# SwiGLU over 8192 x 8192: all loads and stores of the two-row tiles through one DMA queue in a fixed order

## Chip, cores, metric

One core of a Trainium2 chip. The metric is the device time of one execution in microseconds (us), the median of several. The profile is one execution taken by the hardware profiler; "span" is the time from its first to its last instruction, which is 1.7 to 1.9 us shorter than the time of that same execution.

## The reference

```python
x = np.random.randn(8192, 8192).astype(np.float32)
a, b = np.split(x, 2, axis=-1)
return a * (b / (1 + np.exp(-b)))        # out: 8192 x 4096, float32
```

Read 268.4 MB, write 134.2 MB, and do very little with it: a kernel bound by data movement.

## The kernel before

A tile is 256 rows of x, two per partition: 64 KiB per partition to load, 32 KiB to store. There are 32 tiles (`last` is 31) and three slots, each of which holds one tile; ScalarE overwrites b with silu(b), VectorE writes a * silu(b) to the front of the same slot, and the store goes out from there. So the load of tile i+3 needs the slot of tile i, and waits until the store of i has landed.

```python
    R, BUFS = 2, 3
    def load(i, c0=0, cw=R * M):
        inst = nc.sync.dma_start(
            out=slots[i % BUFS][:, c0 : c0 + cw], in_=xv[i * P : (i + 1) * P, c0 : c0 + cw])
        ...
    def store(i, c0=0, cw=R * half):
        eng = nc.scalar if i < last - 1 else nc.sync
        if i % 2 and BUFS <= i < ntiles * 3 // 4:
            eng = nc.gpsimd
        inst = eng.dma_start(
            out=ov[i * P : (i + 1) * P, c0 : c0 + cw], in_=slots[i % BUFS][:, c0 : c0 + cw])
        ...
    for i in range(BUFS):
        load(i)
    for i in range(last):
        ...                      # swiglu(i); tiles 0 to 2 in two halves
        store(i)                 # tile 0 in two pieces
        nxt = i + BUFS
        if nxt < last:
            load(nxt)
        ...                      # the last tile in halves
```

Loads are issued from SP (SyncE), three tiles ahead. Stores are issued from ACT, eleven of them from GpSimd, the last from SP. An issuing engine feeds a queue of its own, called a **ring** below; all rings are served by the same 16 DMA engines (in the profile before, the three rings took 68.6, 19.8 and 11.4% of their time).

## Time and profile before

| | before |
|---|---|
| time, median of the first three runs | 935.39 us (935.17 to 936.15) |
| span of the profiled execution | 934.2 us |
| bytes moved | 402.67 MB |
| VectorE / ScalarE busy | 30% / 24% |

Two longer windows of the steady state show how even it is. The columns are the window, its length, busy time of VectorE, ScalarE and GpSimd with their instructions, the TensorE clock, the share of time in which the 16 DMA engines were busy, and GB/s.

```profile
200.00:316.00 116.00, 34.77 (x5) 28.12 (x4) 1.06 (x2) 1.00 1.00 434
780.00:896.00 116.00, 34.77 (x5) 28.12 (x4) 0.00 (x0) 1.00 1.00 434
```

Share 1.00 and 434 GB/s early and late. The next view is the same table for the last microseconds of the span. A DMA share of 0.06 there is one engine of sixteen. (A packet counts in the window in which it starts, so a short window can exceed 1.)

```profile
928.00:930.00 2.00, 0.00 (x0) 0.00 (x0) 0.00 (x0) 1.00 1.07 459
930.00:932.00 2.00, 0.00 (x0) 0.00 (x0) 0.00 (x0) 1.00 0.71 303
932.00:934.00 2.00, 0.00 (x0) 0.00 (x0) 0.00 (x0) 1.00 0.02 8
```

Nearly all engines stop within two microseconds of one another: from 1.07 to 0.71 to 0.02.

### The profile page before, as it was taken

How to read it: one execution, taken by the hardware profiler on the slowest of the kernel's cores; microseconds unless marked ns; L12 is line 12 of the kernel's file. 1: busy time of each engine (PE TensorE's matmuls, PEld its weight loads, DVE VectorE, ACT ScalarE, POOL GpSimd, SP SyncE). 2: the span in 40 equal slices, each digit the busy share in tenths (PEclk: the TensorE clock that was granted, in tenths of full speed). 3: DMA queues.
4: the chain of work that ended last, by engine and by line, in shares of the span. 5: the costliest groups of instructions: out<-in, count | busy, mean ns of one | idle time of the engine just before them, and what ended most of it. 6: DMA issues, size and time to landing. Idle time of an engine off the chain costs nothing.

```text
span 934.2 us, 219 instructions
## 1 busy us (share of the span) xinstructions
DVE 278.8 (30%) x37; ACT 226.8 (24%) x38; POOL 6.2 (1%) x15
## 2 busy tenths in 40 slices
DVE  0333123332133321333213333133331233312342
ACT  0412320333202333023330233311333113331141
POOL 0000000000000000000000000000000000000000
DMA  9999999999999999999999999999999999999998
GB/s 404 418 426 434 427 441 450 432 427 429 446 414 441 428 443 431 428 434 459 429 413 460 410 446 428 428 446 427 428 429 464 408 429 446 428 446 428 427 428 382
DMA packets 9649, 402.67 MB, mean 431 GB/s; under 512 B 1072, under 2 KB 1072, under 8 KB 1200
## 3 DMA queue, kind: packets, MB, share of 16 engines
q1 hardware_dynamic: 5184, 276.83, 68.6%
q10 hardware_dynamic: 2880, 79.69, 19.8%
q0 software_dynamic: 1584, 46.14, 11.4%
q14 instruction: 1, 0.01, 0.0%
HBM read 268.44 MB, written 134.22 MB: 431 GB/s over the span
## 4 chain that ended last, share of the span: by engine, by line
DMA 70%; issue 12%; DVE 9%; ACT 7%; DVEq 0%; POOL 0%; SPq 0%; POOLq 0%
DMA slot<-in_x_dram 38%; DMA out_dram<-slot 32%; DVE slot L70 9%; ACT slot L66 7%; DVEq L138 0%; POOL out_dram L79 0%; SPq L55 0%; POOLq L79 0%; DVEq L70 0%
## 5 line engine op out<-in xcount | busy, mean ns | idle before, releaser
L70 DVE TENSOR_TENSOR slot<-slot 128x8192 f32<-128x8192 f32 (+2 forms) x37 | 278.8, 7539 | 641.5 <-ACT slot L66 641.2
L66 ACT ACTIVATE slot<-slot 128x8192 f32<-128x8192 f32 (+2 forms) x37 | 225.5, 6105 | 690.1 <-DMA slot<-in_x_dram 690.1
L79 POOL DMA_DIRECT2D out_dram<-slot x11 | 6.0, 544 | 695.6 <-DVE slot L70 695.6
L66 ACT ACT_TABLE_LOAD x1 | 1.3, 1283 | 0.7 <-PEq L127 0.7
L127 POOL MEMSET const-bfloat16-1.0<- 128x1 bf16 x1 | 0.1, 102 | 0.0
L127 POOL MEMSET const-float32-0.0<- 128x1 f32 x1 | 0.1, 99 | 0.2 <-issue 0.2
L127 POOL MEMSET const-float32-1.0<- 128x1 f32 x1 | 0.1, 99 | 0.0
L127 POOL MEMSET const-uint8-127<- 128x1 uint8 x1 | 0.1, 99 | 0.0
## 6 DMA issues: line engine op xcount, KB each, us to landing
out_dram<-slot ACTq DMA_DIRECT2D x18, 4096.0 KB, 32.8
out_dram<-slot POOLq DMA_DIRECT2D x11, 4096.0 KB, 32.6
slot<-in_x_dram SPq DMA_DIRECT2D x2, 4096.0 KB, 29.8
out_dram<-slot SPq DMA_DIRECT2D x1, 4096.0 KB, 19.3
out_dram<-slot SPq DMA_DIRECT2D x2, 2048.0 KB, 14.5
out_dram<-slot ACTq DMA_DIRECT2D x1, 3584.0 KB, 37.5
out_dram<-slot ACTq DMA_DIRECT2D x1, 512.0 KB, 24.6
slot<-in_x_dram SPq DMA_DIRECT2D x31, 38.4
```

Of the source, the lines that this page charges most:

```text
L66: gate = nc.scalar.activation(out=b, in_=b, func=_SILU)
L70: prod = nc.vector.tensor_mul(out=o[:, k0:k1, c0 : c0 + cw], in0=a, in1=b)
L79: inst = eng.dma_start(out=ov[i * P : (i + 1) * P, c0 : c0 + cw], in_=slots[i % BUFS][:, c0 : c0 + cw])
L127: nc = _bacc.Bacc("TRN2", target_bir_lowering=False, num_devices=1)
```

## The change

The intent: fix the order of all transfers by putting them in one ring, as load i+1, store i, load i+2, store i+1, so that each load is followed by the store whose data is ready, and no ring competes with it. The last three stores stand behind the last loads. The special cases for GpSimd and for tile 0 go, and loads run two tiles ahead in place of three.

```diff
     def store(i, c0=0, cw=R * half):
-        eng = nc.scalar if i < last - 1 else nc.sync
-        if i % 2 and BUFS <= i < ntiles * 3 // 4:
-            eng = nc.gpsimd
-        inst = eng.dma_start(
+        inst = nc.sync.dma_start(
...
-    for i in range(BUFS):
-        load(i)
+    load(0)
+    load(1)
     for i in range(last):
...
+        if i == last - 1:
+            swiglu(last, 0, 1)
+        if i + 2 == last:
             load(last, 0, M)
             load(last, M, M)
+        store(i)
+        if i + 2 < last:
+            load(i + 2)
```

More of the change, by code (lines that the diff above doesn't have):

```diff
@@ L59, in load, with swiglu @@
         loads[i].append(inst)
-    def swiglu(i, k0=0, k1=R, c0=0, cw=half, gated=None):
+    def swiglu(i, k0=0, k1=R, c0=0, cw=half):
         rows = slots[i % BUFS].rearrange("p (k s c) -> p k s c", k=R, s=2)
@@ L67, in swiglu @@
         follows_from_others(gate, i, [], [loads, gates, prods, stores])
-        if gated:
-            gated()
         prod = nc.vector.tensor_mul(out=o[:, k0:k1, c0 : c0 + cw], in0=a, in1=b)
@@ L83, in store @@
         stores[i].append(inst)
-    for i in range(BUFS):
-        load(i)
+    load(0)
+    load(1)
     for i in range(last):
-        if i == 0:
-            swiglu(i, 0, 1)
-            swiglu(i, 1, 2, gated=lambda: store(0, 0, half // 4))
-            store(i, half // 4, R * half - half // 4)
-        elif i < BUFS:
+        if i < BUFS:
             for k in range(R):
                 swiglu(i, k, k + 1)
-            store(i)
         else:
             swiglu(i)
-            if i == last - 1:
-                swiglu(last, 0, 1)
-            store(i)
-        nxt = i + BUFS
-        if nxt < last:
-            load(nxt)
-        elif nxt == last:
+        if i == last - 1:
+            swiglu(last, 0, 1)
+        if i + 2 == last:
             load(last, 0, M)
             load(last, M, M)
+        store(i)
+        if i + 2 < last:
+            load(i + 2)
     store(last, 0, half)
```

## The prediction

> **What bounds the kernel now.** I read the head of the profile page first: engine shares, DMA row, traffic.
>
> ```profile
> span 934.2 us, 219 instructions
> ...
> DVE 278.8 (30%) x37; ACT 226.8 (24%) x38; POOL 6.2 (1%) x15
> ...
> DMA  9999999999999999999999999999999999999998
> ...
> DMA packets 9649, 402.67 MB, mean 431 GB/s; under 512 B 1072, under 2 KB 1072, under 8 KB 1200
> ```
>
> VectorE is busy 30% and ScalarE 24%. The DMA engines are at nine tenths or more in 39 of 40 slices, and in the last slice at eight. The question is whether "nine tenths" hides a gap that a better order of transfers could close. So next I took the table of windows for single periods of the steady state (columns: window, its length, busy time of VectorE, ScalarE and GpSimd, clock, DMA share, GB/s).
>
> ```profile
> 200.00:229.00 29.00, 8.69 (x2) 7.03 (x1) 0.00 (x0) 1.00 1.00 434
> 229.00:258.00 29.00, 8.68 (x2) 7.03 (x1) 0.53 (x1) 1.00 1.00 434
> 258.00:287.00 29.00, 8.70 (x2) 7.03 (x1) 0.00 (x0) 1.00 1.00 434
> ```
>
> One tile (a load of 8.39 MB, a store of 4.19 MB) takes 29.0 us, and in it the DMA share is 1.00: there is no gap. 12.58 MB in 29.0 us is 434 GB/s. The timeline confirms the period (columns: start, duration, engine, instruction, in brackets the idle time before it):
>
> ```profile
> 192.48 7.03 ACT L66 ACTIVATE slot<-slot 128x8192 f32<-128x8192 f32 x1 [21.97 <-DMA slot<-in_x_dram]
> 199.54 8.69 DVE L70 TENSOR_TENSOR slot<-slot 128x8192 f32<-128x8192 f32 x1 [20.31 <-ACT slot L66]
> 208.26 0.34 ACTq L79 DMA_DIRECT2D out_dram<-slot  x1
> 221.48 7.03 ACT L66 ACTIVATE slot<-slot 128x8192 f32<-128x8192 f32 x1 [21.97 <-DMA slot<-in_x_dram]
> ```
>
> 221.48 - 192.48 = 29.0 us between activations, of which ScalarE waits 22 for the load. The compute chain from a landed load to a finished product is 7.03 + 8.69, about 15.8 us, half a period.
>
> Last I read the trace's packet records, since shares round. Starts and ends can be strung into 16 strands of serial packets, one per DMA engine. A 64 KiB load packet takes 2.418 us and the next begins about 4 ns before it ends (spacing 2.414); a 32 KiB packet, load or store, takes 1.213 (spacing 1.209); a 16 KiB packet has spacing 0.607, a 4-byte semaphore packet 0.006. From the first packet to the last, about 930.0 us, only one strand has any gap over 30 ns, of 0.3 us. So the bound is the **16 DMA engines' packet rate**, and they never lack work. The long chain of waits (load, ScalarE, VectorE, store, load) is a consequence: each DMA in it is slow because the engines are shared.
>
> **What the Trainium skill says.** "DMA: Bandwidth & Descriptors", section "Issuing engines are not separate DMA queues", says that DMAs issued from ACT, SP and GpSimd run on the same 16 engines and interleave, and that issuing from several saves only sequencer time. The trace agrees: a 32 KiB store packet takes 1.213 us on the ACT, the GpSimd and the SP queue alike. Section "Where 436 GB/s comes from" puts the ceiling at 435.2 GB/s; the steady state measures 434, so at most 0.3% is left. Section "Queues, rings and completion order" says that an engine alternates between rings at packet boundaries; the strands do show load and store packets taking turns. It also says that a completion increment lands only after every earlier write of that engine, and "DMA engines do not wait on semaphores". That matters below.
>
> **The change, part by part.** The bytes, packets, compute instructions and three slots stay.
>
> *Packet work per engine.* Each transfer gives an engine 8 packets. After: 31 loads x 8 x 2.414 = 598.7; the last load in halves, 16 x 1.209 = 19.3; 31 stores x 8 x 1.209 = 299.8; the last store in halves, 16 x 0.607 = 9.7; some 66 semaphore packets x 0.006 = 0.4. Sum **927.9 us**. Before differs only in store 0, sent in pieces: 8 x (0.155 + 1.058) = 9.71 in place of 9.67, a saving of 0.04. On top each engine now loses about 1.6 us to slow packets: 0.7 on the very first, 0.7 at about 55 us. 927.9 + 1.6 = 929.5, against about 930.0 seen. The rest of the span, 934.2 - 930.0 = 4.2 us, is start (the first load is issued at 0.74 and packets flow about 1.4 later) and end (one engine finishes 1.2 after the median, then about 0.9 to the last instruction).
>
> *Issues moved.* 20 issues leave ACT (0.34 each), 11 leave GpSimd (0.53 each). Both wait for loads or products most of the time, so that is worth nothing.
>
> *The single queue: does it run dry?* Its order is load i+1, store i, load i+2, store i+1. Alone on the engines a load lasts 19.3 us (8 packets), a store 9.7. Let load i land at T. Then store i-1 runs to T + 9.7 and load i+1 to T + 29.0. Store i is issued when its product is done, T + 15.8, and its turn comes at T + 29.0: **13 us early**. Load i+2 stands behind it, and needs store i-1 (same slot), landed by about T + 9.7 + 2 = T + 11.7 (the 2 is an estimate, from start latency). So it goes out right after store i, at T + 16.2, 22 us before its turn. No wait reaches the engines.
>
> *Start.* Two loads are issued instead of three. Load 0 lands at 22.6 as before; load 1 keeps the engines until about 42. Store 0 is issued whole after both half products, whose end can be read in the chain of waits before: 30.84 + 4.44 = 35.3. Plus 1.5 to flow is 37, 5 us ahead of need. This is the thinnest margin.
>
> *End.* After the last load only stores 29, 30 and 31 are left, 29 us of transfers, while the products of the last half take about 7 us after its load. No gap, but before had none either, so nothing is gained.
>
> *Sum.* Work -0.04; slow packets between -0.7 (if the stall at 55 us, which falls at the moment ACT issued store 1 at 55.26, goes away) and +0.5; the straggler at the end +-0.5. Span 933.8. The timed median lay 1.2 over the profiled span (935.39 against 934.2), so **935.0 us**.
>
> **The rivals.**
>
> *Order becomes cost: a bubble at each boundary.* With two queues, another ring could fill an engine while one ring waits for the confirmation of its last writes; with one ring nothing fills it. Were each of some 64 boundaries to cost 0.3 us, the time would be 954, the lower edge of "slower". Against it: at the start loads 0, 1 and 2 follow one another in the SP ring alone, and the 4-byte packet between them costs 6 ns; at the end stores 30 and 31 follow load 31 in the SP ring, and the two halves of store 31 run alone there, again with no gap. Only store-then-load in one ring is never shown.
>
> *Pure phases are faster.* If mixing reads and writes cost something, stretches of loads alone and of stores alone would gain. Against: load packets at the start, with no store running, take 2.418 us just as in the mixed steady state, and store packets at the end take 1.213 as in the middle. Even without the two slow spells and with perfect ends the time stays above 932; 2% faster would be 916.7, which is 12 us below the packet sum alone. I see no way to it.
>
> *A wait of the in-order SP sequencer.* A late store now holds the load behind it back. The margins (13 us steady, 5 at the start) speak against it; missing the start's margin wholly costs a few us once, some 938.
>
> **Range and chances.** The packet sum pins the time from below (927.9 + 4.2 + 1.2 = 933.3 with no slow packet), and known run-to-run spread is 935.2 to 936.2. I take 933.2 to 937.0 for 8 in 10; the longer upper side is for small bubbles. Faster by over 2% has 0.01, slower 0.02 (the bubble rival), within 2% 0.97.
>
> **What the changed profile would show.** Steady windows of 29.0 us still at share 1.00 and 434 GB/s. Stores land about 24 us after issue instead of 32.8 (T + 15.8 to T + 39 to 40), while loads take about 42 instead of 38.4 (T + 16.2 to T + 58). SP's own waits move from stores to VectorE, about 28 us per tile, with loads waiting for stores next to nothing. ACT's idle before a gate stays near 22. Store 0 is issued at about 35.3. Wrong would be: gaps over 0.1 us between packets at the change from store to load, a share below 0.99, or packets with other durations than 2.418 and 1.213.

## The result, and the profile after

| | before | after |
|---|---|---|
| median | 935.74 us (4 runs, 935.17 to 936.15) | 940.09 us (4 runs, 939.13 to 941.92) |
| ratio | | 1.0048, 95% interval 1.0034 to 1.0062 |
| span of the profiled execution | 934.2 us | 940.1 us |

A ratio here is the mean time of one kernel's fast runs over the mean of the other's fast runs of the same rounds, so not quite the ratio of the medians. The changed kernel is 0.5% slower, 3 us above the top of the predicted range.

First the parts that came out as predicted. The timeline of one period after (start, duration, engine, instruction; in brackets the idle time before it):

```profile
249.68 7.03 ACT L66 ACTIVATE slot<-slot 128x8192 f32<-128x8192 f32 x1 [22.05 <-DMA slot<-in_x_dram]
256.74 8.69 DVE L68 TENSOR_TENSOR slot<-slot 128x8192 f32<-128x8192 f32 x1 [20.39 <-ACT slot L66]
265.46 0.34 SPq L74 DMA_DIRECT2D out_dram<-slot  x1
265.89 0.38 SPq L55 DMA_DIRECT2D slot<-in_x_dram  x1
278.87 7.03 ACT L66 ACTIVATE slot<-slot 128x8192 f32<-128x8192 f32 x1 [22.16 <-DMA slot<-in_x_dram]
```

The store leaves at T + 15.8 and the load right behind it at T + 16.2, as computed. But the period is 278.87 - 249.68 = 29.19 us in place of 29.00. From the list of DMA issues after (KB each, median us from issue to landing):

```profile
out_dram<-slot SPq DMA_DIRECT2D x31, 4096.0 KB, 23.0
slot<-in_x_dram SPq DMA_DIRECT2D x31, 42.0
```

Predicted were about 24 and 42. The waits of SP's own queue after (waited for, us in total, times, longest):

```profile
SPq L74 <- DVE slot L68: 866.4, 33, 33.6
...
SPq L55 <- DMA out_dram<-slot: 22.0, 1, 22.0
```

SP waits for products, hardly ever for stores to land, so no load is held back. The order does what it was meant to do. Now the DMA row of the page, with the lines beside it, and the tail in the windows:

```profile
DMA  9999999999999999999999999999999999999996
...
DMA packets 9505, 402.67 MB, mean 428 GB/s; under 512 B 1056, under 2 KB 1056, under 8 KB 1056
```

```profile
928.00:930.00 2.00, 0.00 (x0) 0.00 (x0) 0.00 (x0) 1.00 1.01 434
930.00:932.00 2.00, 0.00 (x0) 0.00 (x0) 0.00 (x0) 1.00 0.92 393
932.00:934.00 2.00, 0.00 (x0) 0.00 (x0) 0.00 (x0) 1.00 0.23 98
934.00:936.00 2.00, 0.00 (x0) 0.00 (x0) 0.00 (x0) 1.00 0.19 82
936.00:938.00 2.00, 0.00 (x0) 0.00 (x0) 0.00 (x0) 1.00 0.15 66
938.00:940.00 2.00, 0.00 (x0) 0.00 (x0) 0.00 (x0) 1.00 0.02 8
```

Until 932 us the row is full. Then 0.19 of the engines, 3 of 16, work alone for some 6 us. **Thirteen engines are done at the old time; three are late, and the kernel ends with the slowest.**

The packet records say why. They name no engine, but packets of one engine follow each other about 4 ns short of end to end, so they can be strung into 16 strands, each with the sequence of packets that the program gives every engine. After: thirteen strands end 930.3 to 931.6 us after the first packet, three at 935.9, 936.1 and 937.2. Before: fifteen end at 929.6 to 930.3, one at 931.2. The slowest differs by 937.2 - 931.2 = 6.0, and the spans by 940.1 - 934.2 = 5.9. That is the whole loss of this execution, which was the slowest of the four.

The late strands have no gaps. They have *stretched packets*: 64 KiB load packets that took over 20 ns longer than 2.418 us. After the first 100 us there are 74 in the trace after and 3 in the trace before, and they sit in one place, the eighth packet of a load, the one directly ahead of a store (all excess over 2.418, small ones too, after the first two turns, all strands):

```
packet of a load     1st   2nd   3rd   4th   5th   6th   7th     8th
stretch, ns in sum   489    21     1    30     8    17   518   18747
```

The delay of the slowest strand behind the median one grows fast and then slowly: 2.5 us after load 4, 3.5 after load 7, 4.8 after load 13, 5.8 after load 19, 6.6 after load 28.

Being hit goes with being late. In the traces after, e1_again and e6_all_act together, between 100 and 870 us, the last packet of a load was stretched in 171 of 404 cases in which at least 10 of the other 15 strands were already storing (counted 0.1 us before the packet's ordinary end), and in 64 of 846 cases in which fewer were. Which of the two brings about the other no run tells.

One turn does not fit. At the end, the last two loads follow one another for 38.6 us without a store between them, and stores 29 to 31 come behind them. In after, e1_again and e6_all_act no packet from 872 us of the span on was stretched by more than 15 ns, on any engine. So an unmixed turn can pass without a stall; what the steady turns have besides is open.

### The profile page after: what moved, and what is told of

Same layout as the page of the kernel before. It is cut to its first block, busy times and chain, and to the rows that moved or that the text cites. A ratio compares the mean times of both kernels' runs of the same rounds, so it can differ in the third digit from the quotient of the medians.

```text
span 940.1 us, 219 instructions
## 1 busy us (share of the span) xinstructions
DVE 278.8 (30%) x37; ACT 226.8 (24%) x38; POOL 0.2 (0%) x4
## 4 chain that ended last, share of the span: by engine, by line
DMA 72%; DVE 14%; ACT 11%; SPq 1%; issue 0%; DVEq 0%
DMA slot<-in_x_dram 69%; DVE slot L68 14%; ACT slot L66 11%; DMA out_dram<-slot 2%; SPq L74 1%; DVEq L126 0%; SPq L55 0%; DVEq L68 0%
```

## The experiments

Theory S: an engine that turns from loads to stores is stretched at the turn; hits on the same engines add up, and since each engine has a fixed share of every transfer, its delay is never given back. (The diffs are against the changed kernel unless said otherwise, and abridged.) Rivals: a disturbance of one execution; the shallower prefetch; the SP ring itself; boundaries between transfers in one ring whatever their direction; and, inside theory S, what makes a turn costly.

The table gathers what the packets of nine traces showed; the other runs are told in their sections. A ratio is taken with executions of the kernel before on the same chip in the same rounds. "Stretch per run of loads" is the lengthening of all load packets over 20 ns in the steady state (100 to 870 us), divided by the number of unbroken runs of load packets, per engine. "Late" counts strands that end over 1.5 us behind the median one.

| run | median us | ratio to before | run of loads, us | stretch per run, ns | late | slowest behind median, us |
|---|---|---|---|---|---|---|
| before | 935.74 | | mostly 2.4 | 0.0 | 0 | 1.2 |
| after | 940.09 | 1.0048 | 19.3 | 44 | 3 | 6.7 |
| e1_again | 939.63 | 1.0043 | 19.3 | 61 | 6 | 5.3 |
| e2_store_act | 936.07 | 1.0003 | mostly 2.4 | 0.1 | 0 | 0.6 |
| e3_halves | 941.59 | 1.0062 | 9.7 | 12 | 4 | 2.7 |
| e6_all_act | 940.13 | 1.0046 | 19.3 | 56 | 6 | 4.3 |
| e9_pairs_mended | 940.58 | 1.0053 | 38.6 | 79 | 6 | 4.7 |
| e11_quarters | 947.90 | 1.0130 | 4.9 | 2 | 2 | 3.4 |
| e13_two_rings_in_step | 941.72 | 1.0065 | 19.3 | 41 | 5 | 3.1 |

### Again, unaltered (e1_again)

> The changed kernel once more, unaltered. Theory S (the stall at the switch): in the one ring, the last 64 KiB packet of a load, the one just ahead of the store, is stretched on some engines; an engine hit repeatedly falls behind and ends last. Expected: 939 to 942 us, 1.003 to 1.007 of before, stretched packets (over 2.44 us) almost all the eighth of their load, two to four engines ending 5 to 7 us after the median engine. Rival N (a disturbance of that one profiled execution): the late engines are gone, or the stretched packets lie anywhere in a load.

Measured: 939.63 us, ratio 1.0043 (1.0030 to 1.0056). The tail of this run:

```profile
930.00:932.00 2.00, 0.00 (x0) 0.00 (x0) 0.00 (x0) 1.00 0.96 410
932.00:934.00 2.00, 0.00 (x0) 0.00 (x0) 0.00 (x0) 1.00 0.40 172
934.00:936.00 2.00, 0.00 (x0) 0.00 (x0) 0.00 (x0) 1.00 0.36 156
936.00:938.00 2.00, 0.00 (x0) 0.00 (x0) 0.00 (x0) 1.00 0.10 41
```

Six late engines this time (0.36 of 16), two more than "two to four", the slowest 5.3 us late. Of the 74 packets stretched after the first 100 us, 71 are the last of their load. The rival of a single disturbance falls.

### The stores back on a second ring (e2_store_act)

```diff
-        inst = nc.sync.dma_start(
+        inst = nc.scalar.dma_start(
             out=ov[i * P : (i + 1) * P, c0 : c0 + cw], in_=...
```

> The same order and the same two loads ahead, but the stores are issued from ACT, so that a second ring has work at every switch. Theory S: packets of loads and stores take turns again, no stretched packets after the first 100 us, all engines end within about 1.5 us, 934.5 to 936 us (0.999 to 1.001 of before). Rival D (two loads ahead in place of three, and the order of issue, are to blame): stays at 939 to 941 us.

Measured: 936.07 us, ratio 1.0003 (0.9991 to 1.0016). Its tail:

```profile
930.00:932.00 2.00, 0.00 (x0) 0.00 (x0) 0.00 (x0) 1.00 1.12 475
932.00:934.00 2.00, 0.00 (x0) 0.00 (x0) 0.00 (x0) 1.00 0.02 8
```

No late engine. One load packet in about 3000 runs of loads was stretched in the steady state. Order of issue and depth of prefetch are those of the changed kernel, so neither is to blame: one line undoes the loss.

### Loads in place of the stores (e4_reads)

```diff
+        if i < last - 2:
+            inst = nc.sync.dma_start(
+                out=slots[i % BUFS][:, c0 : c0 + cw], in_=xv[i * P : (i + 1) * P, c0 : c0 + cw])
+        else: ...                # the store as it was
```

> Wrong output on purpose: in tiles 0 to 28 each store is replaced by a load of the same 4 MiB into the same part of the slot, in the same place of the same ring with the same waits; only the last three stores write. Ring, boundaries, completion packets and order are kept, only the change of direction is gone. Theory S: no stretched eighth packets until the last three stores, all engines end within 1.5 us, 933 to 936 us. Rival B (the boundary between two transfers in one ring, whatever their direction): stays at 939 to 942 us with late engines.

Measured (output wrong): 936.33 us, ratio 1.0007 (0.9993 to 1.0021). Its tail:

```profile
930.00:932.00 2.00, 0.00 (x0) 0.00 (x0) 0.00 (x0) 1.00 1.01 434
932.00:934.00 2.00, 0.00 (x0) 0.00 (x0) 0.00 (x0) 1.00 0.23 98
934.00:936.00 2.00, 0.00 (x0) 0.00 (x0) 0.00 (x0) 1.00 0.00 0
```

All engines end within 0.9 us, and of 473 packets of 64 KiB at the end of a load two were stretched, by 31 and 38 ns. (After the first 100 us 40 load packets at other places were, by some 50 ns each, mostly the first or second of a load; they add up to no late engine.) The rival of the bare boundary falls: it takes a change of direction. The time was 0.3 us above the range that was expected.

### The whole ring on ACT (e6_all_act)

The edit replaces `nc.sync` by `nc.scalar` in `load` and in `store`.

> The changed kernel with every load and store on the ACT ring in place of the SP ring. If the stall belongs to one ring changing direction, whichever ring it is: 939 to 942 us with late engines and stretched eighth packets. If the SP ring or SyncE's issue is at fault: 935 to 936 us.

Measured: 940.13 us, ratio 1.0046 (1.0034 to 1.0058), six late engines; all 95 packets stretched after the first 100 us are the last of their load. The SP ring as such is not the cause.

### Half and quarter blocks (e3_halves, e11_quarters)

```diff
-        store(i)
-        if i + 2 < last:
-            load(i + 2)
+        for k in range(R):
+            store(i, k * half, half)
+            if i + 2 < last:
+                load(i + 2, k * M, M)
```

> One SP ring still, but load halves and store halves alternate: 60 switches from load to store in place of 30, and a pause between stores of 9.7 us in place of 19.3. The smaller packets alone add about 2 us by their spacing (8 x 31 x (2 x 1.209 - 2.414) + 8 x 31 x (2 x 0.607 - 1.209)). Theory S with a cost per switch: the late engines fall back about twice as far, 10 to 13 us, 944 to 950 us. Variant S2, the cost grows with the length of the pause in the stores: the lag is as before or less, 937 to 942 us.

Measured: 941.59 us, ratio 1.0062. Twice the turns, but the slowest engine is 2.7 us behind the median in place of 5.3, and the stretch per run of loads is 12 ns in place of 61. A fixed cost per turn is refuted. The time stays at the level of the changed kernel because what the shorter lag gives back, the smaller packets take: the median engine ends 934.2 us after the first packet in place of 930.6.

> One SP ring, quarters of loads and stores alternating: about 120 switches, a pause of 4.8 us between stores. The smaller packets alone add about 7 us by estimate (16 KiB packets at 0.607: 248 x (4 x 0.607 - 2.414) = 3.5; 8 KiB packets at some 0.306 each, not yet measured: 248 x (4 x 0.306 - 1.209) = 3.7). S2: no stretched last packets after the first 200 us and all engines within 2 us, 940 to 943 us. Cost per switch: late engines by over 5 us, 947 us or more.

Measured: 947.90 us, ratio 1.0130. The mechanism came out as S2 said (2 ns per run of loads), the time did not: 5 us over the expected range. The median engine ends 9.1 us later than in e1_again. Of this the packet sizes give 7.2 (the spacing of 8 KiB packets did measure 0.306), and 183 more completion packets per engine give 183 x 0.006 = 1.1, which I had left out. The end of this kernel still loads tile 31 in one run of 19.3 us and then sends store 29 whole. At that turn, 907 us after the first packet, the last one or two of the 16 load packets were stretched on all 16 engines, by 22.9 us in sum, 1.4 per engine; the first packets of that run, for which the ring had waited for a slot, had lost another 3.4 us in sum. So this one turn cost more than all the stretch of loads in the steady state before it, 3.1 us in sum. One strand ends 3.4 us behind the median; where it lost that I have not isolated. Short blocks nearly avoid the stall, and their small packets cost more than it.

### Two loads, then two stores (e5_pairs, e9_pairs_mended)

```diff
+    for i in range(0, last - 3, 2):
+        compute(i); compute(i + 1)
+        store(i);   store(i + 1)
+        load(i + 3); load(i + 4)
```

> One SP ring, but two loads and then two stores at a time: 15 switches from load to store in place of 30, and a pause between stores of 38.6 us in place of 19.3. Cost per switch: the late engines fall back half as far, 2.5 to 3.5 us, 936.5 to 938.5 us. Cost that grows with the pause (S2, which the halves point to): each stall is longer and the total is as after or more, 939 to 943 us.

Measured: 943.84 us, ratio 1.0083. The kernel had a flaw of mine at its end: load 31 waited for store 28 to land with nothing else in the ring. The windows show the hole:

```profile
880.00:885.00 5.00, 0.00 (x0) 5.00 (x1) 0.00 (x0) 1.00 0.88 380
885.00:890.00 5.00, 3.62 (x1) 1.35 (x1) 0.00 (x0) 1.00 0.14 59
```

So its time proves nothing. Its steady state does: 121 of 208 last packets stretched, 147 ns per run of loads. The mended version puts stores 28 and 29 ahead of load 31.

> The pairs again without the hole of their end (there load 31 waited for store 28 with nothing else in the ring; now stores 28 and 29 go ahead of it). Theory S2 (fewer switches, but each pause of the stores 38.6 us long, stalls summed over the engines some 2.4 us per switch as in the first pairs run): no hole, and 938.5 to 941 us, as long as the changed kernel in spite of half the switches. Cost per switch: 936.5 to 938 us.

Measured: 940.58 us, ratio 1.0053 (1.0039 to 1.0068), no hole, six late engines, 79 ns per run. Half the turns, each dearer, the total as in the changed kernel. With runs of loads of 4.9, 9.7, 19.3 and 38.6 us in one ring the stretch per run is 2, 12, 44 to 61, and 79 to 147 ns. In all of these the block of stores that follows grows with the run of loads, so which of the two lengths counts is not told apart. Nor is length all that counts: the last turns above had 38.6 us of loads and no stall, and the one of e11_quarters had 19.3 us and stalled on every engine.

### What must happen at the turn (e7_sbuf, e8_d2d)

In e7_sbuf the store of tiles 0 to 28 becomes a copy to the other half of the slot, in e8_d2d a copy of input to output in DRAM (there the loads also wait for the product).

```diff
+                out=slots[i % BUFS][:, R * half + c0 : R * half + c0 + cw], in_=slots[i % BUFS][:, c0 : c0 + cw]   # e7
+                out=ov[i * P : (i + 1) * P, c0 : c0 + cw], in_=xv[i * P : (i + 1) * P, c0 : c0 + cw]               # e8
```

> Wrong output on purpose: in tiles 0 to 28 the store becomes a copy of the product to the other half of its slot, in the same place of the ring. The engine still turns from reading DRAM to reading the slot, but nothing is written to DRAM. Theory W (the first write to DRAM after a pause stalls the engine): no stretched eighth load packets before the last three stores, all engines within 1.5 us. Theory R (turning from reading DRAM to reading the slot stalls): stretched eighth packets and late engines as in the changed kernel. The total depends on the speed of such copies, which no run has shown yet, so the packets decide, not the time.

Measured (output wrong): 937.57 us, ratio 1.0019. One stretched load packet after the first 100 us, all strands within 1.0 us. Turning from DRAM to the slot as the source is not enough; the steady stall came only where the block behind the load writes to DRAM. (The packets themselves take 2.422 and 1.218 us at the median, a little longer than 2.418 and 1.213, which gives the time.)

> Wrong output on purpose: in tiles 0 to 28 the store becomes a copy of 4 MiB of the input straight to the output in DRAM, in the same place of the ring. The engine never reads the slot, but writes to DRAM after a pause. Theory W: stretched eighth load packets and engines 3 to 7 us late, as in the changed kernel. Theory R: none before the last three stores. Again the packets decide, as the speed of such copies is not known from any run.

Measured (output wrong): 989.00 us, ratio 1.0578. Inconclusive. With reads and writes of DRAM in the same transfers the core moved 533 GB/s at DRAM (268.4 and 134.2 MB, and 29 copies of 4.19 MB read here besides the loads, in 983.8 us), and packets were stretched everywhere: after the first 100 us 1548 of the 32 KiB ones and 494 of the loads, and of the loads mostly the first of its transfer and not the last. The stall at the turn can't be seen in this.

### A trickle of stores across the turn (e10_trickle)

```diff
+            store(i, 0, half // 4, nc.scalar)
+            store(i, half // 4, R * half - half // 4)
```

> The changed kernel, but an eighth of each store (4 KiB packets) goes out on the ACT ring as soon as its product is done, and so takes turns with the load packets up to and over the switch; seven eighths stay in the SP ring in their place. The smaller packets add about 1.2 us (31 x 0.04). If any interleaved store keeps an engine from stalling at the switch: no stretched last load packets after the first 100 us, engines together within 1.5 us, 936 to 937.5 us. If the stall needs the two directions mixed in full, or has to do with the big block of stores that follows: late engines, 940 to 943 us.

Measured: 942.63 us, ratio 1.0073. A miss for the cure: 93 load packets stretched after 100 us, two strands over 7 us behind. The 4 KiB store packets did take turns with the load packets up to the turn, and yet the last load packet of the SP ring was hit (54 of 93 by count as the eighth of its load; the strands of this run could not be strung without swaps, so some of the rest may be miscounted). In one late strand: start in us, ring (1 is SP, 10 is ACT), bytes, stretch in ns:

```
240.12  10   4096    0
240.28   1  65536    0
242.70  10   4096    0
242.85   1  65536  711
245.98   1  28672    0
```

So a few stores between loads do not help, as long as a block of stores follows.

### Two rings, both in the order of the change (e13_two_rings_in_step)

```diff
+        for k in range(R):
+            store(i, k * half, half, nc.scalar if k else nc.sync)
+            if i + 2 < last:
+                load(i + 2, k * M, M, nc.scalar if k else nc.sync)
```

> Every load and every store is cut in two halves; the first halves go through the SP ring, the second through the ACT ring, each in the order of the changed kernel. Two rings are at work at every moment, but both turn from load to store together, so an engine still sees a run of loads of about 19 us and then stores. The smaller packets alone add about 2 us as in the halves. Theory P (the long unmixed run of loads ahead of stores is the cause, whatever the ring): last load packets of the runs stretched, late engines, 941 to 945 us. Theory O (a ring left alone is the cause; a second ring with work covers the switch): no stretched last packets after the first 100 us, engines together, 937 to 939 us. If the rings drift apart so that directions mix, the packets will show it and the run says less.

Measured: 941.72 us, ratio 1.0065 (1.0051 to 1.0078). Its tail:

```profile
932.00:934.00 2.00, 0.00 (x0) 0.00 (x0) 0.00 (x0) 1.00 1.05 451
934.00:936.00 2.00, 0.00 (x0) 0.00 (x0) 0.00 (x0) 1.00 0.63 270
936.00:938.00 2.00, 0.00 (x0) 0.00 (x0) 0.00 (x0) 1.00 0.25 107
```

The rings stayed in step: the strand I followed for two tiles has 16 load packets, alternately of SP and ACT, then 16 store packets. Of 385 runs of exactly 16 load packets, 56 had the last one stretched. Four or five engines are late (0.25 of 16 at the end). Having two rings does not help by itself. Together with e2_store_act this shows: **what costs is that loads and stores come, turn after turn, in unmixed blocks; what a second ring is worth is that it mixes them.**

### The kernel before without GpSimd (e12_before_no_gpsimd)

The edit deletes the two lines that choose GpSimd.

> The kernel before with its eleven GpSimd stores moved to ACT, so two rings in place of three and three loads ahead. If two rings are enough to keep the directions mixed: 935 to 936.5 us, 0.999 to 1.001 of before. If the GpSimd ring was worth something of its own: slower by over 1 us. It is also the one candidate left that might beat the kernel before, but the sum of the packets leaves it at most some 2 us.

Measured: 936.11 us, ratio 1.0004 (0.9991 to 1.0017), no late engine. Two rings out of step are enough; neither this version nor e2_store_act beats the kernel before, and no run did.

## Why the prediction was wrong

*The bound* was right: 16 engines with fixed shares, never idle. After, the median strand ends 930.5 us after its first packet, close to 927.9 of summed packets and some 2.4 of slow ones.

*The margins of the ring* were right. Store 0 was issued at 35.2 us (35.3 predicted), stores 15.8 and loads 16.2 after a landing, and loads waited for stores once.

*The term that failed* is "slow packets between -0.7 ... and +0.5; the straggler at the end +-0.5". The slow packets of the slowest engine measured 8.9 us, some 7.3 more than the 1.6 of an engine before, and the straggler stood 6.7 us behind the median in place of 1.2. The stall at 55 us did not go away either: it moved to the turn ahead of store 0, some 38 us after the first packet, and lengthened one packet on each of the 16 engines by 1.3 us in place of 0.8, which is about the 0.5 us by which the median strand ends later. I took the slow packets for accidents of the first 60 us and carried them over from a kernel that mixes directions, and treated engines as alike, when the end is that of the worst one.

*The rival that came nearest* was "Order becomes cost: a bubble at each boundary". I dismissed it because no gaps appeared where the SP ring had been alone. I looked for the wrong sign, a gap, where the loss shows as a longer packet; at the wrong boundary, as I named store-then-load as the unseen case, when it is load-then-store that costs; and at the end of the kernel, which is no sample of the steady state. The reading itself was right: there the last 11 or so packets of load 31 run alone for 13.3 us, store 30 follows in the same ring, and no packet is stretched by more than 20 ns. But the last turn of the changed kernel has no stall either, while its turns in the middle do, and of those the trace before has none. The mechanism that I gave for it, a ring left alone, is refuted by e13_two_rings_in_step. Whether a completion increment waits for the earlier writes, which the prediction took from the skill for this rival, no run here shows.

*"Pure phases are faster"* was examined from packets inside a phase, and for these it holds: 2.418 and 1.213 us in every kernel with ordinary stores. The cost sits at the edge of the phase.

*What would show it wrong* did: the prediction named packets with other durations than 2.418 and 1.213. The full windows and full DMA row showed little, and that is the trap: the share counts a stretched packet as busy.

*Two slips in its sums* did no harm. 916.7 us lies 11.2 us below the packet sum, not 12. And the 1.2 us from span to median compare the span of one execution with the median of others; within one execution the difference is 1.7 to 1.9 us, so the forecast should have been about 935.6.

Open: why some engines are hit and others never, with different numbers in different executions (three in one, six in two others); why the last turn of these kernels passes without a stall; what in the hardware lengthens the packet; why the delay grows ever more slowly, as if an engine that has fallen far enough behind the others was left in peace; and whether the run of loads or the block of stores sets the size.

## What to carry to other kernels

In a kernel bound by DMA, let loads and stores mix on the engines by giving each a ring of its own that is out of step with the other; strict alternation of big blocks in one order cost 0.5% here, although no engine was ever idle. Judge such a kernel by the slowest of the 16 engines: look at the last microseconds of the DMA share and at packet durations, because a share of 1.00 doesn't tell useful time from stretched packets. When you predict from a sum of packets, ask for each term whether it holds for every engine and in the new neighbourhood.

## What the Trainium skill lacked or had wrong

- "DMA: Bandwidth & Descriptors", section "Issuing engines are not separate DMA queues", says that DMAs issued from several engines interleave, and that issuing so only saves sequencer time. As far as the duration of a packet inside a phase goes the runs agree (1.213 us for a 32 KiB store on every ring). But moving the stores from the SP ring to the ACT ring changed 939.63 to 936.07 us on the same chip, while SP, in the changed kernel, waited for products and not to issue; the section lacks that the interleaving of loads with stores can be worth time.
- No page has the stall at the turn: in one ring, a load packet ahead of a block of stores to DRAM was stretched, on average over engines and turns, by 2, 12, 44 to 61, and 79 to 147 ns after runs of loads of 4.9, 9.7, 19.3 and 38.6 us, on a few engines only, which ended up to 6.7 us late. The last turn, after 38.6 us, had none (after, e1_again, e6_all_act: under 15 ns).
- "DMA: Bandwidth & Descriptors", section "Latency and other measured facts", says that DMA engines 7 and 15 are usually slower and suspects the rings that GpSimd's DMAs use. Here two to six engines were late in kernels without any DMA from GpSimd (e11_quarters: two, e1_again: six). The records name no engine, so whether 7 and 15 were among them is not known.
- "HBM Reference", section "Specifications (TRN2)", gives about 425 GB/s for a core that streams alone; the steady state here, loads and stores together, moved 434 GB/s.
- No page has the single stall at the start: when the first large transfer out of a slot came up, all 16 engines lengthened one load packet, by about 0.8 us before and 1.3 us after. It was there with the copy inside the slot (e7_sbuf, 1.2 us) and with stores on their own ring (e2_store_act, 1.1 us), and absent at that boundary when a load stood in its place (e4_reads).
